# Norm roots from ln, exp and one Newton step, norm steps at other tiles, and the weight factors of FFN tile 0 formed twice

## The chip, the core and the metric

One core of one Trainium2 chip runs the whole kernel. The metric is device time in microseconds (us) of one execution; before the change three runs gave 1977.06, 1984.86 and 1986.21, the median being 1984.86.

## What is computed

One layer of a hybrid decoder on 1040 positions (16 learned ones and 1024 given) of 1024 features, in float32:

```python
u = _rmsnorm(h, norms[l, 0])
p_m, p_r, p_h, p_s = _split(u @ w_in[l], ...)
ys = (y_m, y_r, y_h, y_s)
...
for n_b in range(N_BRANCH):
    gate = jax.nn.sigmoid(u @ w_gate[l, n_b] + b_gate[l, n_b])
    term = gate * (ys[n_b] @ w_branch[l, n_b])
    merged = term if merged is None else merged + term
h = h + _rmsnorm(merged @ w_out[l], norms[l, 1])
u2 = _rmsnorm(h, norms[l, 2])
h = h + _rmsnorm(_conv_ffn(u2, f_up[l], f_conv_w[l], f_conv_b[l], f_down[l]), norms[l, 3])
```

`_rmsnorm` is `x * lax.rsqrt(mean(x*x) + 1e-6) * g`, and `_conv_ffn` is a product with `f_up` (1024 by 5632), a causal convolution over three positions, gelu(gate) times value, and a product with `f_down`. The four mixers that make `ys` lie ahead of everything that is changed.

## The kernel before

Features lie on partitions, positions along the free axis. Every large product is made of three float32r matmuls: `Bulk.split` writes a rounded copy of an operand on ACT (ScalarE; the `h` tile) and the rest on DVE (VectorE; the `l` tile), and `Bulk.mm` multiplies h by h, h by l and l by h. All helpers record their matmuls on L233 (L239 for transposes), all ACT work on L230, all DVE halves of a split on L1192.

The program is written as plain loops. A scheduler sets each engine's order when the kernel is built; it follows the order of writing and `tc.cur_priority`, which `at_priority` moves by a number. On the chip each engine works through its own order and waits at the first instruction that is not ready.

**Branch stage** (L1388 to L1424). For the four groups r, s, m, h and the eight feature tiles n, 18 matmuls go to PSUM and DVE multiplies the three thirds by the sigmoid gate (tile `sb`, L1409). From the second group on, the term is added to `M[n]` (tile `mg`, L1411) on POOL (GpSimd), for n = 3 and 7 on DVE. In the last group each `M[n]` is split for the four position blocks j (258, 256, 256 and 256 columns): 8 tiles times 4 blocks is 32 splits, tiles `mh` and `ml`.

**Projection stage** (L1442 to L1555). For each block j and feature tile n, `proj` makes 24 matmuls with `w_out`; ACT writes them scaled to `z[j]` and squared to `sq[j]`. `chain(j)` is a generator with four steps: sums of squares on PE (a matmul with `ones`), then the root; `spread` on PE, multiply `z` by it (L1482), add the residual (L1483), square on ACT (tile `x`); sums and root of the next norm, and copies of `z` scaled by its weight to `x` on ACT; `spread` again, and the multiplication (L1498). The loop advances the chain of block j-1 ahead of tiles n = 0, 3 and 6 of block j and at the block's end. The root is `Rms.newton`: eleven DVE steps on a 128 by 2 to 4 tile `nt` (L274 to L280), a bit trick and three Newton steps. `spread` (L239) puts the root of each position on all partitions.

`forms(j, pool)` makes the right factors of two blocks in two parts: first `b11`, `b21` (block j alone), then `t1`, `t3`, `b22`, `t2`, `t4`, which need block j+1 too. FA is that of blocks 0 and 1, FB that of blocks 2 and 3.

**FFN up stage** (L1578 to L1655). With seven products in place of eight for a 2 by 2 block product, `up_forms(f)` loads tiles f and 22 + f of `f_up` (tiles `fw`, two buffers), splits the first, and makes `s1` to `s4` and `a22` in ten of 21 slots; `up(f, W, j, F)` makes the seven products of one half of the positions (84 matmuls), puts them together on DVE (L1627 to L1634), and does convolution, gelu and product (L1636 to L1640). Ahead of the loop stand what is left of chains 2 and 3 and FB's second part, with priorities pushed back (L1553). Tiles 0 and 1 go together: factors of both, then half FA of both, then half FB of both.

**Down stage** (L1661 to L1720). Two passes over `f_down`; `finish` makes the last norm for three parts of the positions, the last one after the last matmul.

Of the kernel before, what the change touches and what calls it, by code (L numbers as in the profile page):

```python
# [253 lines left out]
class Rms:  # L254
# [7 lines left out]
    def add(self, s):  # L262
# [28 lines left out]

def rms_of(k, terms, L):
    r = Rms(k, L, len(terms))
    for s in terms:
        r.add(s)
    r.newton()
    return r.spread()
# [930 lines left out]
def build(tc, I, out):  # L1228
# [18 lines left out]
    with k.pool("n1") as xp:  # L1247
# [10 lines left out]
        for x, (a, b) in zip(xs, bt):  # L1258
# [8 lines left out]
            TT(x[:, 0:2], x[:, 0:2], x[:, 2:4], ALU.add)  # L1267
            V.tensor_copy(rs[:, a:b], rms_of(k, [x[:, 0], x[:, 1]], L))
        p = k.ps()
# [117 lines left out]

    M = [bp.tile([128, TQ], F32, name=f"mg{n}") for n in range(KD)]  # L1388
    cm = ExitStack()
    k.use("xmym")  # L1390
    for n_b, g in enumerate(order):
# [7 lines left out]
        for n in range(KD):  # L1399
# [10 lines left out]
            if n_b:  # L1410
                (TT if n % 4 == 3 else G.tensor_tensor)(M[n][:], M[n][:], s[:], ALU.add)  # L1411
            if n_b == 3:
# [4 lines left out]
                if n % 4 == 0:  # L1417
                    for j in range(4):
                        for q in "hl":
                            i = 2 * (n // 4) + "hl".index(q)  # L1420
                            merged[j, n // 4, q] = Q(*((ua, f"q{4 * j + i}") if j < 2 else (mp, f"m{4 * j - 8 + i}")), f"m{q}{j}_{n // 4}")
                for j in range(4):
                    c, a, b = cols(j)
                    B.split(M[n][:, a:b], *(merged[j, n // 4, q][:, n % 4, :b - a] for q in "hl"))  # L1424
    cb.close()
# [43 lines left out]
    def chain(j):  # L1469
# [6 lines left out]
        for i in range(2):  # L1476
            r.add(sq[j][:, i, :L])
        r.newton()
        yield
# [10 lines left out]
        for i in range(2):  # L1490
            r.add(xx[:, i])
        r.newton()
        for n in (2, 3, 4, 5, 6, 7, 0, 1):
# [35 lines left out]
    for j in range(4):  # L1529
        for n in range(KD):  # L1530
            if not j:
                w_out(n)
            if ch and n in (0, 3, 6):
                with at_priority(tc, tc.cur_priority + (0 if n else 30)):
                    next(ch)
            if not n:
                sq[j] = wa.tile([128, 4, HB], F32, tag="sq", name=f"sq{j}")
            proj(n, j)
        if ch:
            next(ch, None)  # L1540
        if j == 1:
            begin(2)
            fa = forms(0, ua)
            FA = next(fa)
        if j == 2:
            next(fa)
            begin(3)
        ch = chain(j)
# [3 lines left out]
    FB = next(fb)  # L1552
    for i, steps in ((46, (ch,)), (88, (ch,)), (125, (ch,)), (126, (ch, fb))):  # L1553
        with at_priority(tc, tc.cur_priority + i):
# [88 lines left out]
    k.use("xm")  # L1643
    for f in range(0, NFF, 2):
        if f in (0, NFF - 2):
            W = [up_forms(f), up_forms(f + 1)]
            for j, F in ((0, FA), (1, FB)):
                for i in range(2):
                    up(f + i, W[i], j, F)
                k.use("xymxymxm")  # L1650
        else:
            for i in range(2):
                W = up_forms(f + i)
                up(f + i, W, 0, FA)
                up(f + i, W, 1, FB)  # L1655
    cf.close()
# [91 lines left out]
```

## Time and profile before

| | us |
|---|---|
| runs | 1977.06, 1984.86, 1986.21 |
| the profiled execution | 1973.67 |
| its span in the profile | 1971.9 |
| PE busy in the span | 1851.5 |
| DVE busy | 1212.9 |
| ACT busy | 742.9 |
| POOL busy | 322.9 |

The page's slices show PE busy nearly throughout, with dips in the mixers, at the end of the branch stage (about 1085 to 1120 us) and between projection and FFN (about 1210 to 1276 us). The granted clock of TensorE falls with the dips. A matmul of 256 or 258 columns follows the one before it after 0.12 us at the full clock and after 0.215 us at half of it; the printed duration of one is longer, since matmuls overlap. A DVE or ACT instruction's printed duration also reaches a little into the next one's, so costs of runs of them are taken from starts.

### The profile page before, as it was taken

What the parts mean: (1) busy time and instruction counts of PE and PEld (TensorE: products, weight loads), DVE (VectorE), ACT (ScalarE), POOL (GpSimd) and SP (SyncE); (2) the same over time, 40 slices, a digit from 0 to 9 for tenths busy, and PEclk for the clock granted to TensorE, in tenths of its full rate; (3) what the DMA queues carried; (4) which work ended last, traced back from release to release, by engine and by line L of the source; (5) the groups of instructions that cost most, each with busy time, mean ns of one, the idle gap of its engine ahead of it and who ended that gap; (6) DMA issues with size and microseconds to landing.
All of it is one profiled execution on the core that took longest, in us unless ns stands there. A gap on an engine that the chain in (4) does not pass through costs nothing.

```text
span 1971.9 us, 33187 instructions
## 1 busy us (share of the span) xinstructions
PE 1851.5 (94%) x13476; PEld 1738.1 (88%) x13476; DVE 1212.9 (62%) x2404; ACT 742.9 (38%) x1138; POOL 322.9 (16%) x235
## 2 busy tenths in 40 slices
PE   7999997989999997989999798499999999999997
PEld 6988997878888997979999798499999999988797
DVE  7566479153363347473157757799999898534445
ACT  4541311121352335543235545444444444323522
POOL 3212216111222225252206100000000000000000
PEclk8999999989999998989999898699999999999998
DMA  4124772664552142223457512122222222445533
GB/s 161 57 68 135 213 219 78 224 165 131 179 156 89 61 151 86 63 90 123 167 179 231 179 44 66 48 68 93 79 81 92 71 81 81 171 146 169 166 123 102
DMA packets 139049, 240.77 MB, mean 122 GB/s; under 512 B 22312, under 2 KB 82256, under 8 KB 138256
## 3 DMA queue, kind: packets, MB, share of 16 engines
q1 hardware_dynamic: 138896, 238.65, 37.6%
q8 instruction: 106, 1.74, 0.4%
q14 instruction: 47, 0.39, 0.1%
HBM read 166.03 MB, written 72.58 MB: 121 GB/s over the span
## 4 chain that ended last, share of the span: by engine, by line
PE 78%; DVE 12%; DMA 3%; ACT 3%; issue 2%; POOL 0%; SPq 0%; DVEq 0%; ACTq 0%; POOLq 0%
PE pm L233 45%; PE px L233 19%; PE py L233 13%; ACT L230 1%; DVE h_qt L786 1%; DVE ml L1192 1%; PE px L239 1%; DMA d<-in_f_down 1%; DMA m_raw<-p_m 1%; DVE ul L1262 0%; DMA h_rg<-p_h 0%; ACT h_e L230 0%; PE py L239 0%; DVE acc L1698 0%; DMA s_ub<-s_su 0%
## 5 line engine op out<-in xcount | busy, mean ns | idle before, releaser
L233 PE MATMUL pm<-uh,w 128*128 128x342 f32 (+2 forms) x2688 | 664.9, 328 | 10.4 <-ACT uh L230 8.3
L233 PEld LDWEIGHTS pm<-uh,w 128*128 128x128 f32 x2688 | 474.6, 192 | 22.4 <-ACT uh L230 8.6
L233 PE MATMUL pm<-ul,w 128*128 128x342 f32 (+2 forms) x1344 | 440.8, 328 | 5.4 <-DVE ul L1262 5.4
L233 PEld LDWEIGHTS pm<-ul,w 128*128 128x128 f32 x1344 | 257.4, 192 | 10.6 <-DVE ul L1262 6.5
L230 ACT ACTIVATE w<-w 128x1024 fp32r<-128x1024 f32 (+2 forms) x111 | 116.3, 1048 | 320.6 <-PE pm L233 267.6
L1192 POOL TENSOR_TENSOR w<-w,w 128x1024 fp32r<-128x1024 f32 (+1 forms) x56 | 141.7, 2530 | 350.1 <-ACT w L230 333.2
L1192 DVE TENSOR_TENSOR w<-w,w 128x1024 fp32r<-128x1024 f32 (+1 forms) x55 | 66.2, 1204 | 55.9 <-ACT w L230 55.8
L230 ACT ACT_TABLE_LOAD x52 | 66.7, 1283 | 7.9 <-DMA s_ys<-s_sy 5.1
L233 PE MATMUL pm<-mh,woh 128*128 128x256 f32 (+1 forms) x192 | 55.1, 287 | 2.4 <-ACT woh L230 2.4
L233 PE MATMUL pm<-ml,woh 128*128 128x256 f32 (+1 forms) x192 | 54.8, 286 | 0.0
L233 PE MATMUL pm<-mh,wol 128*128 128x256 f32 (+1 forms) x192 | 54.4, 285 | 0.0
L1192 DVE TENSOR_TENSOR dl<-d,dh 128x512 fp32r<-128x512 f32 x22 | 15.2, 692 | 59.1 <-ACT dh L230 59.1
L233 PE MATMUL px<-w,dh 128*128 128x512 f32 x132 | 51.5, 396 | 0.0
L233 PE MATMUL pm<-w,dh 128*128 128x512 f32 x132 | 51.2, 395 | 0.0
L233 PE MATMUL pm<-w,drh 128*128 128x256 f32 (+1 forms) x220 | 51.1, 303 | 0.0
L233 PE MATMUL px<-w,drh 128*128 128x512 f32 (+1 forms) x176 | 48.6, 340 | 0.1
L1355 DVE TENSOR_TENSOR sg_h<-pm,rs 128x342 f32<-128x342 f32 x24 | 12.3, 513 | 57.1 <-PE pm L233 57.1
L230 ACT ACTIVATE cg<-zg,fvec 128x512 f32<-128x512 f32 x44 | 35.6, 809 | 22.1 <-DVE zg L1633 21.2
L230 ACT ACTIVATE dh<-d 128x512 fp32r<-128x512 f32 x22 | 13.9, 631 | 70.4 <-PE pm L233 70.2
L230 ACT ACTIVATE cg<-cg 128x512 f32<-128x512 f32 x44 | 27.6, 627 | 31.6 <-DVE cg L1638 31.5
L233 PEld LDWEIGHTS pm<-mh,woh 128*128 128x128 f32 x192 | 36.8, 192 | 3.0 <-ACT woh L230 2.9
L233 PEld LDWEIGHTS pm<-w,drh 128*128 128x128 f32 x220 | 36.0, 188 | 2.1
(775 smaller groups left out, 5151.9 us busy)
## 6 DMA issues: line engine op xcount, KB each, us to landing
fw<-in_f_up SPq DMA_DIRECT2D x44, 512.0 KB
w<-ad SPq DMA_DIRECT2D x43, 512.0 KB
w<-in_w_gate SPq DMA_DIRECT2D x32, 512.0 KB
w<-in_w_in SPq DMA_DIRECT2D x24, 512.0 KB
ad<-cg SPq DMA_DIRECT2D x44, 256.0 KB
d<-in_f_down SPq DMA_DIRECT2D x44, 256.0 KB
r_dw<-r_w SPq DMA_DIRECT2D x17, 256.0 KB
r_db<-r_tb SPq DMA_DIRECT2D x17, 256.0 KB
```

What stands on the lines that cost most here:

```text
L230: return self.nc.scalar.activation(out, in_, f, **kw)
L233: return self.nc.tensor.matmul(out, lhsT, rhs, start=start, stop=stop)
L239: return self.nc.tensor.matmul(out, in_, self.id[:], start=True, stop=True, is_transpose=True)
L786: TT(V3(qt[:, :, o:o + m], w), V3(qt[:, :, o:o + m], w), q.rearrange("p c (m s) -> p c m s", s=4 * B)[:, :, :, 4 * B - w:], ALU.mult)
L1192: (k.nc.vector if engs[1] == "v" else k.nc.gpsimd).tensor_tensor(lo, src, hi, ALU.subtract)
L1355: TT(s[:, a:b], p[:, :b - a], rs[:, Q0 + a:Q0 + b], ALU.mult)
```

## The change

It has five parts. `Rms.root` replaces `newton` in all norms but the first: two ACT functions, Ln and Exp with scale -0.5, give a first value, and four DVE steps one Newton step. `M` becomes four tiles of two feature tiles each, and one split takes two feature tiles of a block at a time (16 splits of 512 or 516 columns). The chain's steps move to tiles n = 0, 2, 5 and 6, FA's second part into tile 6 of block 2, and the third pushed-back step from 88 to 74. The slot counter is set back to 0 after tile 0's factors, so that tile 1's take the same slots. Tile 0's second half is put off: behind tile 8 its factors are loaded and formed again and its FB half is made there.

```diff
+    def root(self):
+        k, m = self.k, self.m
+        V = k.nc.vector
+        t = k.np_.tile([128, 3, 8], F32, tag="nt", name=f"nt{k.n}")
+        v, y, a = (t[:, i, :m] for i in range(3))
+        k.act(y, self.p[:, :m], AF.Ln, scale=1.0 / D, bias=k.eps[:, 0:1])
+        k.act(y, y, AF.Exp, scale=-0.5)
+        V.tensor_scalar(v, self.p[:, :m], 1.0 / D, 1e-6, ALU.mult, ALU.add)
+        V.scalar_tensor_tensor(a, v, -0.5, y, ALU.mult, ALU.mult)
+        V.tensor_tensor(a, a, y, ALU.mult)
+        V.scalar_tensor_tensor(y, a, 1.5, y, ALU.add, ALU.mult)
+        self.y = y
...
-    r.newton()
+    (r.newton if first else r.root)()
...
-                for j in range(4):
+                for j in range(4 * (n % 2)):
                     c, a, b = cols(j)
-                    B.split(M[n][:, a:b], *(merged[j, n // 4, q][:, n % 4, :b - a] for q in "hl"))
+                    B.split(M2[n // 2][:, :, a:b], *(merged[j, n // 4, q][:, n % 4 - 1:n % 4 + 1, :b - a] for q in "hl"))
...
-            if ch and n in (0, 3, 6):
+            if ch and n in (0, 2, 5, 6):
                 with at_priority(tc, tc.cur_priority + (0 if n else 30)):
-                    next(ch)
+                    next(ch, None)
+            if n == 6 and j == 2:
+                next(fa)
...
-        if ch:
-            next(ch, None)
...
-            next(fa)
...
-    for i, steps in ((46, (ch,)), (88, (ch,)), (125, (ch,)), (126, (ch, fb))):
+    for i, steps in ((46, (ch,)), (74, (ch,)), (125, (ch,)), (126, (ch, fb))):
...
-    for f in range(0, NFF, 2):
-        if f in (0, NFF - 2):
-            W = [up_forms(f), up_forms(f + 1)]
-            for j, F in ((0, FA), (1, FB)):
-                for i in range(2):
-                    up(f + i, W[i], j, F)
-                k.use("xymxymxm")
-        else:
-            for i in range(2):
-                W = up_forms(f + i)
-                up(f + i, W, 0, FA)
-                up(f + i, W, 1, FB)
+    W0 = up_forms(0)
+    up(0, W0, 0, FA)
+    slots[0] = 0
+    W1 = up_forms(1)
+    up(1, W1, 0, FA)
+    k.use("xymxymxm")
+    up(1, W1, 1, FB)
+    for f in range(2, NFF - 2):
+        W = up_forms(f)
+        up(f, W, 0, FA)
+        up(f, W, 1, FB)
+        if f == 8:
+            up(0, up_forms(0), 1, FB)
+    W = [up_forms(f) for f in (NFF - 2, NFF - 1)]
+    for j, F in ((0, FA), (1, FB)):
+        for i in range(2):
+            up(NFF - 2 + i, W[i], j, F)
```

What this does to the engines' orders is shown at three places. In the names, the digits behind `nt` and `p` are buffer numbers, a digit or digits behind a factor's `h` or `l` are the tile of `f_up` for left factors (`s1h0`) and the first of the two blocks for right ones (`t1h_2`), and a digit behind `z`, `x2_` or `sq` is the block.

DVE at the end of the projection stage, from `t3` of FA to the first use of chain 2's first root (`nt637`). Before:

```order
L1192 TENSOR_TENSOR t3l_0_10908<-x2_1_10353,t3h_0_10907 128x1032
L1521 TENSOR_TENSOR x2_0_10351<-x2_0_10351,x2_1_10353 128x1032
L280 SCALAR_TENSOR_TENSOR nt637_11223<-nt637_11223 128x2
L1192 TENSOR_TENSOR t2l_0_10912<-x2_1_10353,t2h_0_10911 128x1032
L278 TENSOR_TENSOR nt637_11223<-nt637_11223 128x2
L1467 TENSOR_TENSOR sq3_11236<-sq3_11236 128x2x256
L279 TENSOR_TENSOR nt637_11223<-nt637_11223 128x2
L1192 TENSOR_TENSOR t4l_0_10914<-x2_0_10351,t4h_0_10913 128x1032
```

After the change (its lines are numbered 15 higher or so; L1207 is the split, L1498 the multiplication of `z`):

```order
L1207 TENSOR_TENSOR t3l_0_10860<-x2_1_10317,t3h_0_10859 128x1032
L280 SCALAR_TENSOR_TENSOR nt637_11163<-nt637_11163 128x2
L1483 TENSOR_TENSOR sq3_11170<-sq3_11170 128x2x256
L1537 TENSOR_TENSOR x2_0_10315<-x2_0_10315,x2_1_10317 128x1032
L1207 TENSOR_TENSOR t2l_0_10864<-x2_1_10317,t2h_0_10863 128x1032
L1498 TENSOR_TENSOR z2_10884<-z2_10884,py640_11226 128x4x256 x2
L1207 TENSOR_TENSOR t4l_0_10866<-x2_0_10315,t4h_0_10865 128x1032
```

The root's last step and the multiplication of `z2` now stand ahead of `t4l`; before, four steps of the root were still to come behind `t4l`, and the multiplication came after all of them.

ACT behind the projection stage, at chain 2's second root (`nt644`, after the change):

```order
L230 ACTIVATE x2_2_10851<-z2_10884 128x4x256
L230 ACTIVATE x2_2_10851<-z2_10884,vecs_58 128x256 x7
L230 ACT_TABLE_LOAD
L230 ACTIVATE nt644_11325<-py644_11320,epsv_72 128x2
L230 ACTIVATE x2_2_10851<-z2_10884,vecs_58 128x256
L230 ACT_TABLE_LOAD
L230 ACTIVATE nt644_11325<-nt644_11325 128x2
L230 ACTIVATE p10_0_11565<-px653_11568 128x258
L230 ACTIVATE s1h0_67_11538<-fs0_67_11534 128x512
```

Before, ACT went from the eight scaled copies straight to `p10_0` and `s1h0`; now a load, Ln, a copy, a load and Exp stand between, and so at every root.

PE while chain 3 is being finished. Before, the second sums and the spread of chain 3 are followed by FB's `t1` with tile 0:

```order
L233 MATMUL pm662_11829<-b21h_0_10903,fw2_1_11648 128x258
L239 MATMUL py650_11542<-ident_75,nt649_11529 128x128 x2
L233 MATMUL py651_11554<-ones_59,x2_3_11216 128x1 x4
L239 MATMUL py652_11580<-ident_75,nt651_11559 128x128 x2
L233 MATMUL py668_11931<-t1h_2_11510,s1h0_11622 128x258
```

After the change, the first product that needs chain 3's end (`b22h_2`) and what follows it:

```order
L233 MATMUL pm669_11861<-b21h_2_11436,fw2_1_68_11680 128x258
L233 MATMUL pm672_11905<-b22h_2_11442,s4h1_68_11702 128x258
L233 MATMUL pm674_11982<-b11h_0_10853,fw1_2_69_11944 128x258
L233 MATMUL pm674_11982<-b11l_0_10854,fw1_2_69_11944 128x258
```

Before, five of tile 1's seven FA products were still undone when PE came to `t1h_2`; now all of them, and two of its FB products, stand ahead of `b22h_2`.

## Rows read from the trace of the kernel before

**Rows 1.** Busy time in stretches: branch end, projection, change-over, FFN up, end.

```profile
core 0: us, PE busy (x) PEld busy (x) DVE busy (x) ACT busy (x) POOL busy (x), PEclk, DMA share, GB/s
1085.00:1120.00 35.00, 24.85 (x135) 22.37 (x134) 29.95 (x50) 16.68 (x36) 9.22 (x4) 0.85 0.49 160
1120.00:1210.00 90.00, 90.00 (x761) 89.91 (x760) 51.94 (x105) 44.23 (x90) 0.00 (x0) 1.00 0.18 62
1210.00:1276.00 66.00, 32.17 (x185) 29.59 (x184) 52.85 (x96) 30.44 (x48) 0.00 (x0) 0.66 0.19 65
...
1300.00:1700.00 400.00, 400.00 (x3321) 400.00 (x3320) 357.48 (x673) 185.65 (x318) 0.00 (x0) 1.00 0.25 83
```

**Rows 2.** Timeline of PE, change-over: start, us, what, in brackets idle before and releaser.

```profile
1209.96 0.28 PE L233 MATMUL px<-b11h,fw 128*128 128x258 f32 x1
...
1219.38 1.84 PE L233 MATMUL py<-ones,x 128*128 128x1 f32 x8 [6.51 <-issue]
1223.33 0.58 PE L233 MATMUL pm<-t1h,s1h 128*128 128x258 f32 x1 [2.10 <-ACT s1h L230]
...
1229.81 0.38 PE L239 MATMUL py<-ident,nt 128*128 128x128 f32 x2
...
1244.45 0.66 PE L239 MATMUL py<-ident,nt 128*128 128x128 f32 x2 [6.55 <-DVE nt L280]
1252.95 1.84 PE L233 MATMUL py<-ones,x 128*128 128x1 f32 x8 [7.84 <-issue]
1257.10 0.66 PE L239 MATMUL py<-ident,nt 128*128 128x128 f32 x2 [2.31 <-DVE nt L280]
...
1276.29 0.29 PE L233 MATMUL pm<-t2h,s2h 128*128 128x258 f32 x1
```

**Rows 3.** Timeline of DVE: first and last step of two roots; last split of FB.

```profile
1140.01 0.16 DVE L274 TENSOR_SCALAR nt<-py 128x3 f32<-128x3 f32 x1 [3.78 <-PE py L233]
...
1141.98 0.16 DVE L280 SCALAR_TENSOR_TENSOR nt<-nt 128x3 f32<-128x3 f32 x1
...
1194.53 0.15 DVE L274 TENSOR_SCALAR nt<-py 128x2 f32<-128x2 f32 x1
...
1207.94 0.16 DVE L280 SCALAR_TENSOR_TENSOR nt<-nt 128x2 f32<-128x2 f32 x1
...
1211.59 2.35 DVE L1482 TENSOR_TENSOR z<-z,py 128x1024 f32<-128x1024 f32 x2
...
1269.49 1.23 DVE L1192 TENSOR_TENSOR t4l<-x,t4h 128x1032 fp32r<-128x1032 f32 x1
```

**Rows 4.** Timeline of ACT: Ln and Exp of a mixer, and scaled copies.

```profile
145.92 1.11 ACT L230 ACTIVATE r_rn<-r_rn 128x1088 f32<-128x1088 f32 x1
147.05 1.28 ACT L230 ACT_TABLE_LOAD   x1
148.35 1.11 ACT L230 ACTIVATE r_rn<-r_rn 128x1088 f32<-128x1088 f32 x1
...
1218.59 3.30 ACT L230 ACTIVATE x<-z,vecs 128x256 f32<-128x256 f32 x8 [1.29 <-DVE x L1486]
```

**Rows 5.** Groups of ACT instructions by form: a small one.

```profile
L230 ACT ACTIVATE m_wt<-m_wt,m_cols 16x16 f32<-16x16 f32 x4 | 0.9, 295 | 0.3 <-POOL m_wt L638 0.3
```

**Rows 6.** Tile `mg`: splits on DVE, additions on POOL; one pair beside an addition.

```profile
L1192 DVE TENSOR_TENSOR ml<-mg,mh x32: 405/411/2650, 1081.8 to 1112.2; 128x256 fp32r<-128x256 f32 x24, 128x258 fp32r<-128x258 f32 x8
...
L1411 POOL TENSOR_TENSOR mg<-mg,sb_h x6: 2397/2428/3075, 1077.9 to 1101.7; 128x1026 f32<-128x1026 f32 x6
...
1101.43 2.93 DVE L1192 TENSOR_TENSOR ml<-mg,mh 128x258 fp32r<-128x258 f32 x2
...
1101.68 2.40 POOL L1411 TENSOR_TENSOR mg<-mg,sb_h 128x1026 f32<-128x1026 f32 x1 [1.72 <-DVE sb_h L1409]
```

**Rows 7.** Groups of DVE and ACT, 1300 to 1690 us: one tile's factors.

```profile
L1192 DVE TENSOR_TENSOR fw<-fw,fw 128x1024 fp32r<-128x1024 f32 x19 | 23.2, 1220 | 0.0
...
L1192 DVE TENSOR_TENSOR s1l<-fs,s1h 128x512 fp32r<-128x512 f32 x19 | 13.1, 690 | 16.9 <-PE px L233 9.7 <-PE pm L233 3.6 <-PE py L233 3.6
```

More of the change, by code (lines that the diff above doesn't have):

```diff
@@ L289, in spread, with rms_of @@
         return p[:, :L]
-def rms_of(k, terms, L):
+def rms_of(k, terms, L, first=False):
     r = Rms(k, L, len(terms))
@@ L1267, in build @@
             TT(x[:, 0:2], x[:, 0:2], x[:, 2:4], ALU.add)
-            V.tensor_copy(rs[:, a:b], rms_of(k, [x[:, 0], x[:, 1]], L))
+            V.tensor_copy(rs[:, a:b], rms_of(k, [x[:, 0], x[:, 1]], L, True))
         p = k.ps()
@@ L1386, in cols @@
         return c, TB * j + c, TB * j + HB
-    M = [bp.tile([128, TQ], F32, name=f"mg{n}") for n in range(KD)]
+    M2 = [bp.tile([128, 2, TQ], F32, name=f"mg{n}") for n in range(KD // 2)]
+    M = [M2[n // 2][:, n % 2] for n in range(KD)]
     cm = ExitStack()
@@ L1410, in build @@
             if n_b:
-                (TT if n % 4 == 3 else G.tensor_tensor)(M[n][:], M[n][:], s[:], ALU.add)
+                (TT if n % 4 == 3 else G.tensor_tensor)(M[n], M[n], s[:], ALU.add)
             if n_b == 3:
@@ L1477, in chain @@
             r.add(sq[j][:, i, :L])
-        r.newton()
+        r.root()
         yield
@@ L1491, in chain @@
             r.add(xx[:, i])
-        r.newton()
+        r.root()
         for n in (2, 3, 4, 5, 6, 7, 0, 1):
@@ L1581, in up_forms @@
         B.n += 1
-        g, v = (B.wp.tile([128, D], F32, tag="w0", name=f"fw{c}") for c in (f, NFF + f))
-        gh, gl = (B.wp.tile([128, D], F32R, tag=f"w{i}", name=f"fw{i}_{f}") for i in (1, 2))
+        u_ = f"{f}_{B.n}"
+        g, v = (B.wp.tile([128, D], F32, tag="w0", name=f"fw{c}_{B.n}") for c in (f, NFF + f))
+        gh, gl = (B.wp.tile([128, D], F32R, tag=f"w{i}", name=f"fw{i}_{u_}") for i in (1, 2))
         nc.sync.dma_start(g[:], I["f_up"][f])
@@ L1586, in up_forms @@
         a11, a12, a21, a22 = g[:, :512], g[:, 512:], v[:, :512], v[:, 512:]
-        s = T_("s", 0, 512, f"fs{f}")[:]
+        s = T_("s", 0, 512, f"fs{u_}")[:]
         o = {}
         def cut(n, src):
-            h, l = slot(f"{n}h{f}"), slot(f"{n}l{f}")
+            h, l = slot(f"{n}h{u_}"), slot(f"{n}l{u_}")
             B.split(src, h[:], l[:])
```

## Prediction

> **What bounds the kernel now.** I read the stretches first, then PE's own timeline in the stretch that dips, then the engines it waits for. In the FFN stage PE is busy 400 of 400 us, a matmul every 400/3321 = 0.120 us at full clock [rows 1]; nothing that leaves PE's work alone can gain there. The same holds for the projection, 90 of 90 us. What is open lies in two stretches that the change touches. From 1085 to 1120 us PE is busy 24.9 of 35 us, at a clock of 0.85. From 1210 to 1276 us it is busy 32.2 of 66 us at a clock of 0.66. Its timeline there shows four long waits that hang on norm chains 2 and 3: 6.5 us before the second sums of chain 2, 6.6 us before the spread of chain 3's first root, 7.8 us before its second sums, 2.3 us before its last spread [rows 2]. So the chain from the last projection product to FB's factors is the bound, and what PE can do meanwhile is the cover.
>
> **How the sums are taken.** The profiled execution took 1973.67 us with a span of 1971.9. The median of the runs is 1984.86, 11.2 us above it, so I carry the gain worked out in the profile over to the median. A difference of under 0.5%, 9.9 us, can't be told from none.
>
> **The root by itself.** Eleven DVE steps take 1141.98 + 0.16 - 1140.01 = 2.13 us when DVE is free [rows 3]. In the new root a table load stands before Ln and another before Exp. The trace has that pair in a mixer: Ln, a load of 1.28 us, Exp, each starting 0.02 us after the end of the one before [rows 4]. A small ACT function takes 0.295 us [rows 5]. With the first load done while ACT waits for the sums, a root is 0.3 + 1.28 + 0.3 + three dependent DVE steps at 0.2 (11 steps in 2.13) + two hand-overs of about 0.1 = 2.7 us. So it is 0.6 us longer where nothing else runs, and shorter only where its steps queue among others: chain 2's first root took from 1194.53 to 1208.10, 13.6 us, its eleven steps lying between FA's splits [rows 3]. Four steps meet fewer.
>
> In the projection each of the first four roots has 33 or 34 matmuls between sums and spread, 3.9 to 4.1 us. ACT's queue there holds at most a scaled copy of 0.41 [rows 4] and one projection output beyond the 2.7, so I charge 0.4 us in all, for the third root, where an output is squared between Ln and Exp. Bounds: 0, and 3 us if each is late by 0.75.
>
> A rule of the Trainium skill (ScalarE: Activation LUTs, What ACT_TABLE_LOAD costs) says that a switch costs a drain of about 1.38 us on top of the load. The mixer's rows show 1.28 us between Ln and Exp and no more, so the trace does not bear it out. By the page every root would be 2.8 us longer. The Trainium skill (same page, Table sets: the hidden batching unit) also has Ln and Exp in one set, one load for both; the mixer's pair has a load between, and so has the new order.
>
> **Branch end, 1085 to 1120 us.** 32 splits of about 0.41 us become 16 of 0.69 (the 512-column split of [rows 7]). That is 13.1 us against 11.0, but the 32 took far more than 13.1: two of them beside a POOL addition took 2.93 us and ended when it did [rows 6], and their maximum is 2.65. Five additions have splits behind them before, some 8 us lost; after the change splits come in three batches, so three or four additions do. DVE is full here, 30.0 of 35 us, all of it up to 1112, and gate multiplications that PE waits for stand behind the splits. The order puts 8 of 16 splits ahead of the last of these where it was 24 of 32; but five DVE steps then lie between it and the last split that the first projection product needs, 5.3 us instead of 4.0 by starts. I take 2.3 us gained. Bounds: 2 lost (two more blocked batches of 2.4 each, less half a batch saved) and 6 gained (most of the 10.2 us of idle).
>
> **Change-over, 1210 to 1276 us: when the chain gets on.** All times are on the clock of before.
>
> - Chain 2's first root now ends within FA's splits and its spread stands 56 matmuls ahead of the projection's end, 1209.96 - 6.7 = 1203.3. The multiplication starts 8 us earlier than 1211.59 [rows 3], but FA's `t4l` and two sums of squares are placed before the end of that step, and the last of these waits for the last projection tile. Second sums at about 1213.6 instead of 1219.38 [rows 2].
> - Chain 2's second root has ACT's seven copies (7 x 0.41 = 2.9 us), two loads, an eighth copy and two functions in line: 1212.9 + 2.9 + 1.28 + 0.3 + 0.41 + 1.28 + 0.3 = 1219.3. `s1h` of tile 0 stands behind it, so PE starts tile 0's `t1` at 1220 to 1221 against 1223.33, and the spread comes at 1224.4 instead of 1229.81 [rows 2].
> - Chain 3's first root: its sums follow at once; Ln, `b11h` (1032 columns, 1.1 as for 1088 [rows 4]), Exp, then three DVE steps among tile 1's. Spread at 1236.7 instead of 1244.45. Its multiplication, residual, squares and sums then queue with tile 0's convolution; second sums at 1249.3 instead of 1252.95.
> - Chain 3's second root: eight copies, `s4h`, `a22h`, load, Ln, tile 2's split (1024 columns, 1.1), load, Exp. Its last step comes at 1257.3, spread at about 1258, where it was 1257.10 [rows 2]. Here the lead is eaten. The multiplication then stands behind five DVE steps of tiles 1 and 2, and FB's last split ends at about 1275 instead of 1269.49 + 1.23 = 1270.7 [rows 3].
>
> **What PE has done by then.** Before, PE reaches 1276.29 with 153 FFN matmuls done since 1209.96 [rows 2] (by the order, 160 rows less seven of sums and spreads). After the change, up to FB's `t4` with tile 1, it is 278: half FA and FB of tile 1, half FA of tile 0, two products of tile 2 and the start of a third. Allowing for three done early before, that is 122 more, 122 x 0.12 = 14.6 us of full-speed work brought into a stretch that stood idle. PE, part of the time at half clock (0.215 us per matmul), is through them at about 1279 instead of 1276.29 + 14.6 = 1290.9. That is 11.9 us; I take 11, since DVE is nearly full right behind it (357 of 400 us [rows 1]). Bounds: 5 if FB comes another 6 us later, 16 if chain 3 ends when it did.
>
> **Tile 0's factors again.** One set of factors is 1.22 + 9 x 0.69 = 7.4 us of DVE [rows 7], six copies on ACT and two loads of 512 KB. DVE idles 42.5 us of the 400 [rows 1], 16.9 us of it before `s1l` alone, for PE [rows 7], and a tile's factors are made one tile ahead. A tile is 168 matmuls, 20.2 us, in which DVE is busy 357.5 x 20.2 / 400 = 18.1 us; less 7.4 that is 5.3 per half. So the half-tile put off has 7.4 + 5.3 = 12.7 us of DVE against 10.1 us of PE, 2.6 us too much, mostly in stock. Charge 0.5, bounds 0 and 2.6. The matmuls are the same in number.
>
> **End.** The last root lies on the path: 2.7 against 2.1 us, charge 0.5.
>
> Sum: -2.3 - 11 + 0.4 + 0.5 + 0.5 = -11.9, say 12 us: 1961.7 for the profiled execution, 1973 as a median.
>
> **The rivals.**
>
> 1. *ACT becomes the chain's bound.* 23 table loads more are 29.5 us of ACT. For it: every root of chains 2 and 3 stands in line behind copies and splits, and DVE, which works in order, waits at the root's second step. If FB's factors come 10 us later than before rather than 5, the 14.6 us are spent waiting and the gain is 4 to 8 us: about 1979, which reads as no change. Against it: ACT is busy 30 of 66 us there [rows 1]. The drain that the Trainium skill states (ScalarE: Activation LUTs, What ACT_TABLE_LOAD costs) would lead here too: three exposed roots at 2.8 us are 8 us.
> 2. *The lead is not eaten.* If copies and splits are passed quicker than I line them up and FB is ready by 1271, 16 us come here and up to 6 at the branch end: 1965.
> 3. *Slower: PE stands at the spreads of the projection.* PE works in order, and today it is covered for 90 of 90 us [rows 1]. If a root takes not 2.7 but 9 us there (loads behind `z` and `sq` outputs that themselves wait for PE), each of four is 5 us late: 4 x 5 = 20 us, and the clock falls as at 1210, a few us more. Against 12 gained that is 1996. It decides once a root there takes over 3.9 us; the order has at most one output between sums and Exp, which speaks against it.
> 4. *A change that does nothing* is excluded: the orders differ as shown.
>
> **Chances.** Forecast (gain 8 to 16) 0.58, of which 0.10 fall short of 9.9 us; rival 1, 0.26; rival 2, 0.10; rival 3, 0.06. So faster 0.48 + 0.10 = 0.58, same 0.10 + 0.26 = 0.36, slower 0.06. The range runs from rival 2's 1965, less 3 for the spread of the runs, to no gain at all, 1985: it leaves out rival 3 and the ends.
>
> **What would show it.** From 1210 on: second sums of chain 2 within 5 us of the projection's end, its second root's Exp 6 us behind, PE's idle time down from 34 to 22 to 26 us, and no wait of PE before `t1` with tile 1 that is longer than 6 us. Two loads per root and no drain. 1120 to 1210 still without idle time. At tile 8 no PE wait over 2.6 us. PE idle by over 2 us at spreads of the projection, or FB's `t4l` more than 10 us behind its old place, would make it wrong.

## The result, and the profile after

Four runs of the changed kernel gave 1961.44, 1954.57, 1969.74 and 1962.74 us, a median of 1962.09; four of the kernel before, the three shown and 1982.93, have a median of 1983.89. The ratio on record is 0.9896 (the two medians alone give 0.9890), with a 95% interval of 0.985 to 0.9942: faster by 1.0%, between 12 and 30 us. The profiled execution has a span of 1959.7 against 1971.9, so 12.2 us less.

The stretches of [rows 1] in the changed kernel, same columns:

```profile
core 0: us, PE busy (x) PEld busy (x) DVE busy (x) ACT busy (x) POOL busy (x), PEclk, DMA share, GB/s
1085.00:1120.00 35.00, 27.44 (x161) 26.00 (x161) 29.99 (x40) 19.40 (x29) 12.18 (x5) 0.85 0.55 177
1120.00:1210.00 90.00, 89.12 (x748) 88.31 (x747) 48.72 (x67) 58.42 (x109) 0.00 (x0) 1.00 0.17 62
1210.00:1276.00 66.00, 46.12 (x287) 43.84 (x287) 54.57 (x86) 44.52 (x70) 0.00 (x0) 0.79 0.28 89
1300.00:1700.00 400.00, 400.00 (x3290) 398.46 (x3289) 360.30 (x675) 190.91 (x319) 0.00 (x0) 1.00 0.27 87
```

In the change-over PE now makes 287 matmuls where it made 185, and idles 19.9 us instead of 33.8. In the projection it idles 0.88 us, where it idled not at all, most of it at two spreads by PE's waits from 1120 to 1215 us (in total, times, longest):

```profile
PE py L239 <- DVE nt L280: 0.7, 2, 0.4
```

The third root shows why, in the timelines of PE and ACT (its sums, its first load, its spread):

```profile
1167.27 0.95 PE L233 MATMUL py<-ones,sq 128*128 128x1 f32 x8
1168.66 1.28 ACT L230 ACT_TABLE_LOAD   x1
1172.74 0.40 PE L239 MATMUL py<-ident,nt 128*128 128x128 f32 x2 [0.40 <-DVE nt L280]
```

The sums are done at 1168.22 and the load starts at 1168.66, behind a squared output, so both loads of the root lie between sums and spread.

The FFN stage is full as before, with tile 0's factors formed twice. The timeline of PE shows where the change-over's idle time lies now, the counterpart of [rows 2]:

```profile
1215.47 1.02 PE L233 MATMUL py<-ones,x 128*128 128x1 f32 x8 [0.93 <-issue]
1221.91 0.58 PE L233 MATMUL pm<-t1h,s1h 128*128 128x258 f32 x1 [5.41 <-ACT s1h L230]
...
1225.87 0.63 PE L239 MATMUL py<-ident,nt 128*128 128x128 f32 x2
...
1238.27 0.38 PE L239 MATMUL py<-ident,nt 128*128 128x128 f32 x2
...
1247.90 0.39 PE L233 MATMUL pm<-t2h,s2l 128*128 128x258 f32 x1 [3.69 <-DVE s2l L1207]
1251.22 1.84 PE L233 MATMUL py<-ones,x 128*128 128x1 f32 x8 [1.45 <-issue]
1260.23 0.38 PE L239 MATMUL py<-ident,nt 128*128 128x128 f32 x2
1265.62 0.47 PE L233 MATMUL pm<-b22h,s4h 128*128 128x258 f32 x1 [3.80 <-ACT b22h L230]
...
1280.20 0.28 PE L233 MATMUL px<-t4h,a22l 128*128 128x258 f32 x1
```

The two waits for chain 3 of 6.6 and 7.8 us are down to none and 1.45. What is left are waits for factors: tile 0's `s1h`, tile 1's `s2l`, FB's `b22h`. The last row is the 278th FFN matmul; in the kernel before, the 278th is this one:

```profile
1290.85 0.28 PE L233 MATMUL py<-b21l,fw 128*128 128x258 f32 x1
```

ACT's timeline at chain 2's second root, with the two loads of one root:

```profile
1214.68 2.90 ACT L230 ACTIVATE x<-z,vecs 128x256 f32<-128x256 f32 x7 [1.29 <-DVE x L1502]
1217.60 1.28 ACT L230 ACT_TABLE_LOAD   x1
1218.89 0.26 ACT L230 ACTIVATE nt<-py,epsv 128x2 f32<-128x2 f32 x1
1219.05 0.50 ACT L230 ACTIVATE x<-z,vecs 128x256 f32<-128x256 f32 x1
1219.57 1.28 ACT L230 ACT_TABLE_LOAD   x1
1220.86 0.20 ACT L230 ACTIVATE nt<-nt 128x2 f32<-128x2 f32 x1
...
1221.24 0.62 ACT L230 ACTIVATE s1h<-fs 128x512 fp32r<-128x512 f32 x1
```

The sums are done at 1216.5, but the first load starts only at 1217.60, behind seven copies, and `s1h`, for which PE stands 5.41 us, is behind all of it. Each ACT function starts 0.01 us after the end of its load. The drain of about 1.38 us per switch that the Trainium skill states (ScalarE: Activation LUTs, What ACT_TABLE_LOAD costs) is not in these rows. On DVE the root's first step stands too, and FB's last split comes 7.0 us later than in [rows 3]:

```profile
1219.19 0.16 DVE L277 TENSOR_SCALAR nt<-py 128x2 f32<-128x2 f32 x1 [3.82 <-ACT nt L230]
...
1221.10 0.16 DVE L278 SCALAR_TENSOR_TENSOR nt<-nt 128x2 f32<-128x2 f32 x1 [1.15 <-ACT nt L230]
...
1276.53 1.24 DVE L1207 TENSOR_TENSOR t4l<-x,t4h 128x1032 fp32r<-128x1032 f32 x1
1277.68 0.69 DVE L1207 TENSOR_TENSOR s1l<-fs,s1h 128x512 fp32r<-128x512 f32 x1
```

The last root of the span, sums and spread, first in the kernel before and then in the changed one:

```profile
1957.76 1.44 PE L233 MATMUL px<-ones,fs 128*128 128x1 f32 x8 [1.68 <-DVE fs L1693]
1961.41 0.69 PE L239 MATMUL py<-ident,nt 128*128 128x128 f32 x2 [2.22 <-DVE nt L280]
```

```profile
1945.72 1.05 PE L233 MATMUL px<-ones,fs 128*128 128x1 f32 x8 [1.70 <-DVE fs L1714]
1949.32 0.69 PE L239 MATMUL pm<-ident,nt 128*128 128x128 f32 x2 [2.55 <-DVE nt L280]
```

**A finer measure.** Runs of one kernel spread over 15 us, so parts of a few us can't be read from medians alone. The tile views give first and last starts, and from these each profile can be cut into stretches. Of the kernel before, tiles `mg`, `z` and `cg`:

```profile
L1411 POOL TENSOR_TENSOR mg<-mg,sb_s x6: 2401/2408/2420, 1032.2 to 1047.8; 128x1026 f32<-128x1026 f32 x6
...
L230 ACT ACTIVATE z<-pm,vecs x32: 454/476/479, 1112.7 to 1210.2; 128x256 f32<-128x256 f32 x24, 128x258 f32<-128x258 f32 x8
...
L1638 DVE SCALAR_TENSOR_TENSOR cg<-zg,fvec,cg x44: 742/746/754, 1241.8 to 1704.2; 128x512 f32<-128x512 f32 x44
```

And of the changed kernel:

```profile
L1427 POOL TENSOR_TENSOR mg<-mg,sb_s x6: 2002/2402/2414, 1036.4 to 1051.8; 128x1026 f32<-128x1026 f32 x6
L1207 DVE TENSOR_TENSOR ml<-mg,mh x16: 678/680/2490, 1087.6 to 1112.6; 128x512 fp32r<-128x512 f32 x12, 128x516 fp32r<-128x516 f32 x4
...
L230 ACT ACTIVATE z<-pm,vecs x32: 452/474/479, 1112.5 to 1211.7; 128x256 f32<-128x256 f32 x24, 128x258 f32<-128x258 f32 x8
...
L1654 DVE SCALAR_TENSOR_TENSOR cg<-zg,fvec,cg x44: 736/745/753, 1243.6 to 1693.4; 128x512 f32<-128x512 f32 x44
```

The same cut for all profiles of this study. *Begins*: first POOL addition of the branch stage; *branch*: from there to the first projection output; *projection*: to its last output; *t4l*: from that to FB's last split; *gates*: from the last projection output to the last FFN convolution step on `cg`; *rest*: from that to the end of the span; *whole*: from *begins* to the end.

| profile | begins | branch | projection | t4l | gates | rest | whole |
|---|---|---|---|---|---|---|---|
| before | 1032.2 | 80.5 | 97.5 | 59.3 | 494.0 | 267.7 | 939.7 |
| changed | 1036.4 | 76.1 | 99.2 | 64.8 | 481.7 | 266.3 | 923.3 |
| changed_again | 1048.8 | 76.2 | 99.4 | 65.1 | 481.9 | 266.3 | 923.8 |
| keep_ffn_order | 1047.6 | 75.5 | 99.3 | 55.8 | 489.8 | 266.7 | 931.3 |
| ffn_order_alone | 1037.3 | 81.1 | 96.7 | 69.8 | 486.9 | 266.4 | 931.1 |
| newton_everywhere | 1034.0 | 75.7 | 97.8 | 70.5 | 487.6 | 266.4 | 927.5 |
| single_splits | 1037.7 | 80.7 | 97.9 | 64.9 | 481.7 | 266.2 | 926.5 |
| old_chain_places | 1033.4 | 75.3 | 98.2 | 64.4 | 481.3 | 266.2 | 921.0 |
| v_before_ln | 1037.3 | 75.9 | 99.5 | 66.9 | 484.3 | 266.4 | 926.1 |
| more_put_off | 1036.7 | 75.4 | 99.4 | 64.2 | 492.0 | 266.5 | 933.3 |
| sqrt_newton | 1032.4 | 75.6 | 97.6 | 58.8 | 474.8 | 265.3 | 913.3 |
| sqrt_alone | 1037.6 | 75.9 | 99.0 | 49.3 | 468.7 | 263.9 | 907.5 |
| sqrt_alone_old_places | 1032.2 | 74.8 | 97.7 | 50.8 | 469.9 | 263.9 | 906.3 |
| sqrt_alone_old_ffn | 1038.9 | 75.4 | 99.0 | 41.7 | 475.0 | 264.8 | 914.2 |

So the change is worth 939.7 - 923.3 = 16.4 us from the branch stage on: 4.4 in the branch, 12.3 behind the projection, 1.4 at the end, less 1.7 in the projection. The 12.2 of the spans are less by 4.2, because in the changed kernel's profile the branch stage happened to begin 4.2 us later, behind work whose order is the same. The kernel before was profiled once, so how far its stretches repeat is not known. One sign that they may not repeat to the last us: *rest* is 1.0 to 1.5 us shorter than before in every profile without Sqrt, also in ffn_order_alone and keep_ffn_order, which share none of the five parts of the change.

### The profile page after: what moved, and what is told of

It is laid out like the page before. It is cut to its first block, busy times and chain, and to the rows that moved or that the text cites. A ratio compares the mean times of both kernels' runs of the same rounds, so it can differ in the third digit from the quotient of the medians.

```text
span 1959.7 us, 33119 instructions
## 1 busy us (share of the span) xinstructions
PE 1857.5 (95%) x13476; PEld 1745.7 (89%) x13476; DVE 1205.3 (62%) x2310; ACT 780.3 (40%) x1173; POOL 319.9 (16%) x235
## 4 chain that ended last, share of the span: by engine, by line
PE 78%; DVE 12%; ACT 4%; DMA 3%; issue 2%; POOL 0%; SPq 0%; DVEq 0%; ACTq 0%; POOLq 0%
PE pm L233 43%; PE px L233 20%; PE py L233 14%; ACT L230 2%; DVE h_qt L801 1%; DMA m_raw<-p_m 1%; PE px L239 1%; DVE ul L1277 0%; DMA h_rg<-p_h 0%; ACT h_e L230 0%; DVE acc L1719 0%; DVE ml L1207 0%; DVE h_kt L785 0%; ACT x L230 0%; DVE h_qa L801 0%
## 5 line engine op out<-in xcount | busy, mean ns | idle before, releaser
L233 PEld LDWEIGHTS pm<-uh,w 128*128 128x128 f32 x2688 | 476.9, 193 | 21.8 <-ACT uh L230 7.8
L1207 POOL TENSOR_TENSOR w<-w,w 128x1024 fp32r<-128x1024 f32 (+1 forms) x56 | 140.5, 2509 | 350.5 <-ACT w L230 337.5
L1207 DVE TENSOR_TENSOR w<-w,w 128x1024 fp32r<-128x1024 f32 (+1 forms) x55 | 66.3, 1205 | 59.5 <-ACT w L230 59.5
L233 PE MATMUL px<-w,drh 128*128 128x256 f32 (+1 forms) x220 | 57.2, 326 | 0.0
L1207 DVE TENSOR_TENSOR dl<-d,dh 128x512 fp32r<-128x512 f32 x22 | 15.2, 692 | 58.9 <-ACT dh L230 58.8
L1370 DVE TENSOR_TENSOR sg_h<-pm,rs 128x342 f32<-128x342 f32 x24 | 12.3, 513 | 55.7 <-PE pm L233 55.7
L233 PE MATMUL pm<-w,drh 128*128 128x256 f32 (+1 forms) x176 | 42.2, 310 | 0.8 <-DVE w L1207 0.8
L233 PEld LDWEIGHTS px<-w,drh 128*128 128x128 f32 x220 | 37.2, 188 | 4.1
```

Source lines behind the costliest of these rows:

```text
L233: return self.nc.tensor.matmul(out, lhsT, rhs, start=start, stop=stop)
L1207: (k.nc.vector if engs[1] == "v" else k.nc.gpsimd).tensor_tensor(lo, src, hi, ALU.subtract)
L1370: TT(s[:, a:b], p[:, :b - a], rs[:, Q0 + a:Q0 + b], ALU.mult)
```

## The experiments

**How far a profile repeats.** The changed kernel, once more, with no edit.

> The changed kernel once more, to see how far a stretch of the profile repeats. Theory (the work before the branch stage differs from execution to execution, the stages behind it hardly do): from the branch stage's first POOL addition to the end within 1 us of 923.3, the start of that stage anywhere from 1032 to 1048. Rival: the stages behind it vary by several us too, and differences of 2 to 4 us between single profiles say nothing.

Median 1962.2, ratio 0.9916 (0.9886 to 0.9946). The span was 1972.6, 12.9 us longer than in the first profile, yet *whole* was 923.8 against 923.3, and no stretch differed by over 0.3. Of the difference, 12.4 us lie ahead of the branch stage. The theory holds, on this one repeat of one kernel; differences of 2 us and more in *whole* are read on its strength, and sums of experiments are made with it.

**The FFN order taken out.**

```diff
-    W0 = up_forms(0)
-    up(0, W0, 0, FA)
-    slots[0] = 0
...
+    for f in range(0, NFF, 2):
+        if f in (0, NFF - 2):
+            W = [up_forms(f), up_forms(f + 1)]
...
```

> The changed kernel with the old order of FFN tiles 0 and 1 (both halves of both tiles in turn, factors of tile 0 formed once, no slot reset); roots, pairs and chain places stay as changed. Theory (the gain in the change-over is PE work brought into the wait for FB): only FA's two half-tiles, some 150 to 170 FFN matmuls, are there before FB's t4l, so PE's idle time between 1210 and 1300 rises from 20 us to over 30 and the time by 8 to 13 us, to 1970 to 1975; ratio to the kernel before 0.993 to 0.997. Rival (the gain comes from the chain getting on earlier): at most 3 us lost, 1962 to 1965, ratio 0.989 to 0.991.

Median 1977.14, ratio 0.9985 (0.9956 to 1.0014): nearly all the gain of the medians is gone. *Whole* is 8.0 us longer, all of it behind the projection, although FB's last split came 9 us earlier after the last projection output (55.8 against 64.8). PE's idle time, in 90 us from 1.7 us ahead of the last projection output, is 29.8 us against 19.9, so the theory is met at the low end of its 8 to 13 us. PE needs not only an early FB but work ahead of it. PE's timeline of this kernel shows it standing for chain 3 and FB again:

```profile
1259.58 1.84 PE L233 MATMUL py<-ones,x 128*128 128x1 f32 x8 [10.15 <-issue]
1265.90 0.66 PE L239 MATMUL py<-ident,nt 128*128 128x128 f32 x2 [4.48 <-DVE nt L280]
1271.24 0.58 PE L233 MATMUL py<-t1h,s1h 128*128 128x258 f32 x1 [4.68 <-ACT t1h L230]
```

Why there was no work is in DVE's timeline of the same kernel:

```profile
1278.16 1.23 DVE L1207 TENSOR_TENSOR t4l<-x,t4h 128x1032 fp32r<-128x1032 f32 x1
1279.31 0.69 DVE L1207 TENSOR_TENSOR s1l<-fs,s1h 128x512 fp32r<-128x512 f32 x1
1280.09 0.69 DVE L1207 TENSOR_TENSOR s3l<-fw,s3h 128x512 fp32r<-128x512 f32 x1
```

Tile 1's factors come right behind FB's last split. Eleven of the 21 slots come from one pool (`ffe`), ten from another (`ffl`). Tile 0 takes ten, tile 1 stands in the second pool from its second slot on, and in DVE's order that is filled only behind FB's last split. The changed kernel's reset lets tile 1 use tile 0's ten slots, so its factors are split from 1238 to 1254; there it is tile 2's `s1l` that comes right behind FB (1277.68 above). The reset and the half that is put off were taken out together; neither was tried alone.

**The FFN order alone**, put into the kernel before (the same lines the other way round, and the names of `up_forms`).

> The kernel before with only the new order of FFN tiles 0 and 1 (tile 1 in the slots of tile 0, tile 0's FB half put off and its factors formed again). Taken out of the changed kernel the order cost 8.0 us. Theory (its worth is tile 1's factors getting slots before FB, and does not hang on the root): from the branch stage's first POOL addition to the end 939.7 - 8 = 931 to 933 us; the time 5 to 9 us below the kernel before, ratio 0.995 to 0.9975. Rival (with eleven DVE steps per root tile 1's factors push chain 3 back on a full DVE, and the gain needs the short root): 4 us or less gained, 936 us or more, ratio 0.998 or above.

Median 1971.89, ratio 0.9957 (0.9928 to 0.9986). *Whole* is 931.1: 8.6 us gained, so the theory holds. FB's last split came 10.5 us later than before, and *gates* still fell by 7.1; most of the other 1.5 lies in *rest*.

**More work put off.** Tile 1's FB half goes behind tile 12 in the same way.

```diff
-    up(1, W1, 1, FB)
...
         if f == 8:
             up(0, up_forms(0), 1, FB)
+        if f == 12:
+            up(1, up_forms(1), 1, FB)
```

> The changed kernel with tile 1's FB half put off as well (behind tile 12, its factors formed again there). Theory (after the change PE waits in the change-over for the factors of tiles 0 to 2, on DVE and ACT, and no longer for FB alone; so more work that FB is not needed for brings little): the stretch from the last projection output to the last FFN gate within 2 us of 481.7, the time 1960 to 1964. Rival (cover is still what is short): that stretch shrinks by 4 to 8 us, to 474 to 478, the time to 1954 to 1958.

Median 1973.75, ratio 0.9986 (0.9961 to 1.0011); *gates* 492.0, so 10.3 us lost. Neither expected this. PE's timeline has one long wait, and ACT's, below it, says for what:

```profile
1277.68 0.58 PE L233 MATMUL px<-t3h,s3h 128*128 128x258 f32 x1 [16.44 <-ACT s3h L230]
```

```profile
1276.99 0.63 ACT L230 ACTIVATE s3h<-fw 128x512 fp32r<-128x512 f32 x1 [1.30 <-DVE t4l L1207]
```

This is tile 2's `s3h`, held until FB's last split. With tile 1's FB half gone, the work next in line is tile 2's, and tile 2 has no slot. In the changed kernel tile 1's FB products lie there, and they can start one by one as FB's factors come. Work counts as cover only if it has memory.

**The old root in the changed kernel.**

```diff
-    (r.newton if first else r.root)()
+    r.newton()
...
-        r.root()
+        r.newton()
...
-        r.root()
+        r.newton()
```

> The changed kernel with eleven DVE steps for every root again, the rest as changed. Theory (the new root is dearer where DVE is free and cheaper only where its steps queue): the chain's milestones after 1210 move by under 2 us either way, the time stays within 1960 to 1966, ratio to the kernel before 0.988 to 0.991. Rival (the root is the gain): chain 2's first root takes 13 us again and FB's t4l comes 5 us or more later; 6 to 12 us lost, 1968 to 1974.

Median 1963.08, ratio 0.9913 (0.9879 to 0.9947). The medians can't tell it from the changed kernel; *whole* says 4.2 us lost: 5.9 behind the projection, less 1.4 gained in the projection, where PE idles not at all again. FB's last split comes 5.7 us later. So the root is worth some 4 us, more than the theory allowed and less than the rival. PE's longest wait, before chain 3's second sums:

```profile
1261.50 1.83 PE L233 MATMUL py<-ones,x 128*128 128x1 f32 x8 [12.20 <-issue]
```

**The splits of one tile in the changed kernel.**

```diff
-                for j in range(4 * (n % 2)):
-                    B.split(M2[n // 2][:, :, a:b], ...)
+                for j in range(4):
+                    B.split(M[n][:, a:b], ...)
```

> The changed kernel with 32 splits of one tile each in the branch stage again, the rest as changed. Theory: the stretch from the first POOL addition of the branch stage to the first projection output goes back from 76 to 80 us, so 4 us lost, 1964 to 1968, ratio 0.990 to 0.993. Rival (the two profiles differ there by chance): that stretch stays within 1 us of 76, no time lost.

Median 1967.02, ratio 0.993 (0.9898 to 0.9961). *Branch* is 80.7, as in the kernel before (80.5): 4.6 us lost there, 1.3 won back in the projection, 3.2 in all. The theory holds for the stretch that it named.

**The chain's old places in the changed kernel.**

```diff
-            if ch and n in (0, 2, 5, 6):
+            if ch and n in (0, 3, 6):
...
-    for i, steps in ((46, (ch,)), (74, (ch,)), (125, (ch,)), (126, (ch, fb))):
+    for i, steps in ((46, (ch,)), (88, (ch,)), (125, (ch,)), (126, (ch, fb))):
```

> The changed kernel with the chain's steps at the old places (tiles 0, 3, 6 and the end; second factors of FA behind the last tile; 88 instead of 74), the rest as changed. Theory: chain 2's second sums come at 1219 instead of 1215.5 and all of chain 3 behind them, FB's t4l 3 to 5 us later, and as PE has run out of work by then the time rises by 3 to 5 us, to 1965 to 1967. Rival (FB's factors stand behind DVE's queue anyway): t4l within 1 us of 1276.5, no time lost.

Median 1954.49, ratio 0.9877 (0.9839 to 0.9915); *whole* 921.0, 2.3 us less. The theory falls: FB's last split comes 64.4 us after the last projection output, with the new places 64.8. Chain 2's multiplication of `z` starts 6.5 us ahead of that output here (1200.37, output at 1206.9) and 6.0 ahead in the changed kernel. With the short root the step is early enough from either place.

**One set of tables.** Sqrt and a reciprocal in place of Ln and Exp.

```diff
-        k.act(y, self.p[:, :m], AF.Ln, scale=1.0 / D, bias=k.eps[:, 0:1])
-        k.act(y, y, AF.Exp, scale=-0.5)
+        k.act(y, self.p[:, :m], AF.Sqrt, scale=1.0 / D, bias=k.eps[:, 0:1])
+        V.reciprocal(y, y)
```

> The changed kernel with Ln and Exp of the new root replaced by Sqrt on ACT and a reciprocal on DVE; the Newton step stays. Sqrt alone needs a table load only when another set was in use before, so 19 of the 75 loads go, with one small ACT function per root less and one DVE step per root more. Theory (ACT's queue with its loads sets when the second roots end): each of the four exposed roots ends 1.3 to 2.8 us earlier, the stretch from the last projection output to the last FFN gate shrinks from 481.7 to 476 to 479 us, the time by 3 to 6 us, to 1956 to 1959; ratio to before 0.986 to 0.988. Rival (DVE's queue sets it, the loads lie beside it): that stretch within 1.5 us of 481.7.

Median 1953.77, ratio 0.987 (0.9831 to 0.9908). *Whole* is 913.3, 10.0 us less: 6.9 behind the projection, 1.6 in it, 1.0 at the end, 0.5 in the branch. The theory holds and was too small. The edit takes away 19 of the 75 loads (56 are left) and one small ACT function per root, and adds one DVE step; these were not parted. Then without the Newton step:

```diff
-        V.tensor_scalar(v, self.p[:, :m], 1.0 / D, 1e-6, ALU.mult, ALU.add)
-        V.scalar_tensor_tensor(a, v, -0.5, y, ALU.mult, ALU.mult)
-        V.tensor_tensor(a, a, y, ALU.mult)
-        V.scalar_tensor_tensor(y, a, 1.5, y, ALU.add, ALU.mult)
```

> The same with no Newton step: the root is Sqrt on ACT and one reciprocal on DVE, in place of two ACT functions and four DVE steps. Theory (ACT sets the root's end): like the kernel with the Newton step, within 1 us. Rival (DVE's queue sets it: each further DVE step of a root waits behind others): another 3 to 5 us less than with the Newton step, the stretch from the last projection output to the last FFN gate at 472 to 475 us.

Median 1948.15, ratio 0.985 (0.9808 to 0.9892). *Whole* is 907.5, another 5.8 less, so here the rival holds, and was too small too: both queues set the root's end, ACT's with its loads and DVE's with its steps (two more loads go as well, 56 to 54). The groups of ACT count the loads, first of the changed kernel, then of this one:

```profile
L230 ACT ACT_TABLE_LOAD x75 | 96.2, 1283 | 7.1 <-DMA s_ys<-s_sy 3.6 <-DMA h_rg<-p_h 1.4 <-PEq L1762 0.7
```

```profile
L230 ACT ACT_TABLE_LOAD x54 | 69.3, 1283 | 7.2 <-DVE s_ys L1169 3.6 <-DMA h_rg<-p_h 1.9 <-PEq L1758 0.7
```

Copies and squares between the roots bring no load, so one serves all roots up to the first gelu. Ln and Exp, in turn, needed one each in every root: 22 for 11 roots, and one more beside the gelus. By the Trainium skill (ScalarE: Activation LUTs, Table sets: the hidden batching unit) activations are to be batched by set, which these counts bear out; that Ln and Exp share a set and need one load is not what this kernel's rows show. From 1.5 us ahead of the last projection output (1212.5) on, 66 us of this kernel:

```profile
1211.00:1277.00 66.00, 55.33 (x386) 52.79 (x385) 59.72 (x93) 37.70 (x64) 0.00 (x0) 0.84 0.20 64
```

PE idles 10.7 us, where it idled 19.9 in the changed kernel; DVE is busy 59.7 of 66 and is now the fuller queue.

**The mean square ahead of Ln.** DVE's 3.82 us at L277 looked like a cost by itself: that step only reads the sums, as Ln does, but comes behind it.

```diff
+        V.tensor_scalar(v, self.p[:, :m], 1.0 / D, 1e-6, ALU.mult, ALU.add)
-        k.act(y, self.p[:, :m], AF.Ln, scale=1.0 / D, bias=k.eps[:, 0:1])
+        k.act(y, v, AF.Ln)
```

> The changed kernel with the root's first DVE step (mean square plus epsilon) ahead of Ln, and Ln reading its result; nothing else differs. In the changed kernel this step stands 3.8 us on DVE for Ln, which is in line on ACT behind seven copies and a load. Theory (DVE's standing there holds up tile 0's first factors and with them PE's 5.4 us before t1 with s1): that wait of PE falls to 2 to 3 us, the time by 2 to 3 us. Rival (DVE then stands as long at the next step, for Exp): PE's wait there stays at 5 to 6 us and the time within 1.5 us of the changed kernel's.

Median 1964.95, ratio 0.9928 (0.9901 to 0.9955); *whole* 926.1, 2.8 us more. PE's wait before `t1` with `s1` stays at 5.36 us, as the rival has it; the time does not stay within the rival's 1.5 us. DVE's step no longer stands for ACT, in DVE's timeline:

```profile
1217.53 0.16 DVE L275 TENSOR_SCALAR nt<-py 128x2 f32<-128x2 f32 x1 [1.16 <-PE py L233]
...
1222.31 0.16 DVE L278 SCALAR_TENSOR_TENSOR nt<-nt 128x2 f32<-128x2 f32 x1 [1.09 <-ACT nt L230]
```

It bought nothing, since `s1h` stands in ACT's queue behind the loads. A new wait of PE, at the last spread, costs more; what in the order brought it was not tried:

```profile
1266.92 0.66 PE L239 MATMUL py<-ident,nt 128*128 128x128 f32 x2 [9.18 <-DVE nt L280]
```

**Does a shorter chain make the FFN order needless?** Sqrt alone, with the old order of tiles 0 and 1.

> The kernel with Sqrt and reciprocal as root, and the old order of FFN tiles 0 and 1 besides. The order was worth 8 us (931.3 against 923.3) where FB's last factor came 65 us after the last projection output; now it comes after 49 us. Theory (the order's worth is the work it puts before FB, so it shrinks with the wait): 2 to 5 us more than 907.5, so 909 to 912. Rival (its worth is in tile 1's factors getting slots early, whatever the chain does): the full 8 us, 915 to 916.

Median 1954.88, ratio 0.9879 (0.9835 to 0.9922). *Whole* is 914.2, 6.7 us more, between theory and rival and nearer to the rival. FB's last split comes 41.7 us after the last projection output and the order is still worth 6.7.

**The best version**: sqrt alone with the chain's old places, both edits as above.

> The kernel with Sqrt and reciprocal as root, and the chain's steps at the old places besides (tiles 0, 3, 6 and the end). With the root from Ln and Exp the old places cost nothing (921.0 us from the branch stage's first POOL addition to the end against 923.3). Theory (the places do not matter once a root is short): within 2 us of the 907.5 of the new places, a time of 1946 to 1950. Rival (the old places are the better ones): 3 us or more less, 1942 to 1945.

Median 1942.28, ratio 0.9823 (0.9779 to 0.9867), the fastest of all. *Whole* is 906.3, within 2 us of 907.5: by the stretches the theory holds, though the median lies at the rival's end. Who takes this root over has to weigh its accuracy. The Trainium skill (ScalarE: Activation LUTs, Precision budgets) gives up to 58 ULP (units in the last place) for Sqrt on inputs from 1 to 2, and here no Newton step follows; no profile shows the error.

## Why the prediction was right, and where it fell short

- **What bounds the kernel.** As predicted: the chain from the last projection product to FB, and what PE can do meanwhile. Of 16.4 us, 12.3 came behind the projection, and the FFN order alone brings 8.6, of which 7.1 there.
- **Change-over, forecast -11 (bounds -5 to -16).** The 278th FFN matmul was forecast at about 1279 against 1290.9 and came at 1280.20 against 1290.85, 10.7 us earlier on the profiles' clocks; counted from the last projection output 12.3 us fell away in *gates*. PE's idle time was forecast at 22 to 26 us and was 19.9. The milestones came 1.5 to 3 us late, most of it because the last projection output came 1.5 us late: second sums 1215.47 (forecast 1213.6), Exp's end 1221.06 (1219.3), spreads 1225.87 (1224.4), 1238.27 (1236.7) and 1260.23 (1258), end of FB's last split 1277.8 (1275). Chain 2's multiplication of `z` came 5.9 us earlier than before (1205.66), not 8. That the lead is eaten held. What the prediction counted but didn't name is the slots: by keep_ffn_order and more_put_off, matmuls are there ahead of FB only for a tile whose factors have memory by then.
- **Branch end, forecast -2.3 (+2 to -6).** The term was mis-sized: 80.5 to 76.1, so 4.4, and single_splits gives back 4.6. The mechanism was right: three splits beside an addition took 2.07 to 2.49 us, where five had taken 1.11 to 2.65. Over the usual time of a split that is 4.6 us lost instead of 8.7, which makes nearly all of the 4.4.
- **Projection waits, forecast +0.4 (0 to 3).** *Projection* grew by 1.7, within the bounds, but the step behind the 0.4 failed. It had a root of 2.7 us, its first load done while ACT waits for the sums, and 0.4 for one root. The first load started from 0.1 us ahead of the sums' end to 0.4 us behind it, after an output or a copy in ACT's queue, and the first four roots took 4.1 to 4.5 us from the end of the sums to the spread. So all four outlasted their cover: by starts, each spread came 0.36 to 0.68 us after the matmul ahead of it, where the pace is 0.12, which is 1.5 us together.
- **Tile 0's factors again, forecast +0.5 (0 to 2.6).** No cost seen: PE busy 400 of 400 us.
- **End, forecast +0.5.** From the start of the sums to the spread it took 3.60 us (1945.72 to 1949.32) against 3.65, but not because the root is as short: PE stood 2.55 us for it, before 2.22, so it is 0.33 longer even here, where the first load ran while PE made the sums. The eight sums hid that: they took 1.05 us instead of 1.44, at a granted clock of 0.87 against 0.57 in the 3.8 us of sums and root.
- **The root by itself.** Two loads and no drain, as forecast. Its price of 2.7 us is near the 2.55 at the end of the span and too low by 1.4 to 1.8 in the projection; behind it, in queues, the root is worth more than that costs, 4.2 us in all against eleven steps, but a root with one table set and one step would have been worth 15.8 more.
- **The sum.** -11.9 was forecast, -16.4 came, by *whole*; the missing 4.5 are 2.1 of the branch, 1.3 of the change-over, 0.5 and 0.7 of tile 0's factors and the end, and 1.2 between the last gate and the last square that no term named and that was not traced (it lies in *rest*, and may be one of the single profile of before), less 1.3 in the projection. The median fell by 21.8 us, outside the gain of 8 to 16 that the forecast's chance was given to, and lies 0.1 us above the low end of the range, 1962. That it lies inside is luck: four runs spread over 15 us. Over the repeat's runs the median fell by 15.3 (1977.54 to 1962.2), nearer to the stretches. Carrying the profiled execution's gain over to the median hid 4.2 us, since the stages ahead of the change do not repeat.
- **The parts.** Taken out singly, FFN order, root, pairs and places cost 8.0, 4.2, 3.2 and -2.3, in sum 13.1. Of the 3.3 us that are left to 16.4, about 1 lies in *rest*, which no part taken out gave back; the others may come from parts that help each other, which was not tried. The places, which the prediction gave part of chain 2's lead, have none beside the new root; beside the old one they were not tried.
- **The rivals.** ACT as the chain's bound was half true: FB's last split came 7.0 us later, short of the 10 that this rival needed, and 19 loads less, with one ACT function less per root, took 6.9 us off *gates*. Rival 2 had a price of 1965, nearest to the measured median, but what it needs did not come: FB was ready at 1277.8, not by 1271. That PE stands at the spreads of the projection was seen, at four spreads, with 1.5 us and not the 20 of this rival.

## What to carry to other kernels

When PE waits for a chain, count not only the work that could go ahead but whether its operands have memory before the chain ends; setting a slot counter back and forming factors a second time was worth more here than every shortening of the chain in the change. A root, or any small function on a chain, costs its places in the queues: give it the fewest table loads and the fewest steps, and look for a function whose set stays loaded. And cut profiles at fixed events before comparing kernels: here that turned a difference of 12.9 us between two profiles of one kernel into one of 0.5.

## What was not expected of the hardware

The stages ahead of the branch, whose order is the same in all profiles, took from 1032.2 to 1048.8 us. A lower granted clock of TensorE goes with the late starts: from 400 to 600 us it was 0.97 in the kernel before and 0.88 in the repeat of the changed kernel, with 1416 and 1278 matmuls done at nearly the same busy time. In keep_ffn_order, which began at 1047.6, it was 0.89. Why the same order got different clocks is not shown. The rows, first of before:

```profile
400.00:600.00 200.00, 191.45 (x1416) 168.99 (x1414) 94.62 (x163) 63.80 (x103) 45.88 (x35) 0.97 0.52 155
```

and of the changed kernel run again:

```profile
400.00:600.00 200.00, 191.71 (x1278) 167.54 (x1277) 88.77 (x146) 58.47 (x90) 41.59 (x32) 0.88 0.49 146
```

The other surprise is that DVE's first step of the root came behind Ln on ACT, though it needs only the sums, as Ln does. L277 starts at 1219.19, 0.04 us after Ln's end (1218.89 + 0.26), and it stands behind Ln's end in all eight roots of chains 0 to 3, in six of them by 0.04 us or less. Ln and this step read the same sums in PSUM and also write into the same tile `nt`; which of the two makes the order is not shown. The kernel with the step put first does not tell, as Ln reads the step's result there.
